# Order of the score products inside one attention item of a decoder-layer kernel

## The chip, the cores and the metric

One core of a Trainium2 chip runs the whole kernel. The time is in device microseconds (us) of one execution; the kernel before was run three times for its median, and one further execution was taken by the hardware profiler. All rows below come from that profiled execution.

## What is computed

One decoder layer for a prompt of 2048 tokens (width 1024) and a small sample group. The part that matters here is the dilated attention of the prompt: 8 heads of 64 dimensions, three patterns `p` (dilation 1, 4 and 16). In each pattern a block of 128 queries sees its own block of 128 keys and, where there is one, the block before:

```python
scores = jnp.einsum('bnqchd,bnkchd->bnchqk', qb, kb).astype(jnp.float32) * (HEAD_DIM ** -0.5)
scores = jnp.where(valid[None, :, None, None], scores + bias[None, None, None], NEG)
m = jnp.max(scores, axis=-1, keepdims=True)
p = jnp.exp(scores - m)
l = jnp.sum(p, axis=-1, keepdims=True)
out = jnp.einsum('bnchqk,bnkchd->bnqchd', (p / l).astype(v.dtype), vb)
```

Before it come the input projection, norms and the pooling mixer; after it the merge of the patterns, the output projection and a convolutional feed-forward network (up-projection, convolution, down-projection).

## The kernel before, in words

The kernel runs in stages: projection, then attention, then output projection, then the feed-forward network. Attention is cut into 192 **items**, 24 for each head (eight for each pattern). An item `(h, p, pr)` is two query blocks, `s = 0` and `s = 1`. Both write into one PSUM tile `Sp` of 128 x 2 x 256 fp32 values, one half for each `s`. A half is 256 wide where the block has an earlier block of keys and 128 wide where it has none; these are called wide and narrow here. The queries of patterns 1 and 2 are copied beforehand into `qs` by GpSimd (L241).

Three functions issue the work of an item, and `advance(i)` (the body of the loop over items) calls them for three different items: `scores` of item i, `turn` of item i - 2, `values` of item i - 3. So a result of `scores` is first needed by TensorE two items later.

- `scores` (L275 to L296): for each half two products into `Sp`, with the high (L289) and the low part (L290) of the keys; then one VectorE instruction (L292) that adds the bias table, writes `T` and takes the row minimum into `st` (with a short second instruction that reads the accumulator); then the exponential on ScalarE (L294) into `Pt`.
- `turn` (L298 to L309): a transpose on TensorE (L302) for each 128 x 128 block of `Pt`, two to four in an item, into a PSUM tile `tp`, then one copy to SBUF, `PTs`: on VectorE (L305) three times of four, on ScalarE (L307) the fourth.
- `values` (L311 to L333): for each block a product of `PTs` with the values (L324, two instructions in the trace for each one in the code); after every second item a ScalarE copy of the result (L328), and a store of `O` to DRAM after each group of four (L227 to L233).

The first eight items are issued while the stage before ends, and the scheduler of the framework may reorder them. All others stand in a loop under `tc.manual_schedule()`, which keeps the order of the program on every engine. The framework adds the semaphores by itself and follows the use of tiles. `Sp` has four buffers, `T` three, `Pt` three, `tp` and `Op` share four, `PTs` has four.

In the same loop the SyncE queue (SP) issues loads: keys and queries of the next head (L161 to L166), values (L185, L193), and late in the stage eight pieces of the output weights, `rawo` (L737), each of which is split by ScalarE (L112) and VectorE (L113) right where it stands in the program order; the first stands at item 150, the sixth of head 6.

Of the kernel before, what the change touches and what calls it, by code (L numbers as in the profile page):

```python
# [47 lines left out]
def kernel(ctx, tc, ins, cst, outs):  # L48
# [212 lines left out]
    def views(h, p, idx):  # L261
        r = DILS[p]
        blk, c = divmod(idx, r)
        lo = blk - 1 if blk else 0

        def keys(x):
            if p == 0:
                return x[:, lo * P:(blk + 1) * P]
            return x.rearrange("p (m c i) -> p m c i", c=r, i=RUN)[:, lo * P // RUN:(blk + 1) * P // RUN, c, :]

        return queries(h, p, idx), keys(heads[h][1]), keys(heads[h][2]), ([idx - r] if blk else []) + [idx]
# [3 lines left out]
    def scores(it):  # L275
        h, p, pr = it
        tab = heads[h][3]
        if pr % 4 == 0:
            state["st", p] = pq.tile([P, 8], F32, tag="st", name="st", bufs=8)
        st = state["st", p]  # L280
        Sp = psum.tile([P, 2, 2 * P], F32, tag="mm", name="Sp", bufs=4)
        Pt = pq.tile([P, 2, 2 * P], F32, tag="P", name="Pt", bufs=3)
        blocks = []
        for s in range(2):
            idx = 2 * pr + s
            i8 = idx % 8
            q, kh, kl, kb = views(h, p, idx)
            w = P * len(kb)
            nc.tensor.matmul(Sp[:, s, :w], q, kh, start=True, stop=False)  # L289
            nc.tensor.matmul(Sp[:, s, :w], q, kl, start=False, stop=True)  # L290
            T = pq.tile([P, 2 * P], F32, tag="T", name="T", bufs=3)
            nc.vector.tensor_tensor_reduce(out=T[:, :w], in0=Sp[:, s, :w], in1=tab[:, p, 2 * P - w:], op0=ALU.add,  # L292
                                           op1=ALU.min, scale=1.0, scalar=3e38, accum_out=st[:, i8:i8 + 1])
            nc.scalar.activation(Pt[:, s, :w], T[:, :w], AF.Exp, bias=st[:, i8:i8 + 1], scale=-1.0)  # L294
            blocks += [(s, idx % 4, n, b, len(kb)) for n, b in enumerate(kb)]
        return st, Pt, blocks  # L296

    def turn(it, res):  # L298
# [57 lines left out]
    def advance(i):  # L356
        if i >= AHEAD:
            spread_next(i + SPREAD)
        if i < len(items):
            attn[i] = scores(items[i])  # L360
        if 0 <= i - 2 < len(items):
            PTs[i - 2] = turn(items[i - 2], attn[i - 2])
        if 0 <= i - 3 < len(items):
            values(items[i - 3], attn.pop(i - 3), PTs.pop(i - 3))
# [380 lines left out]
    with tc.tile_pool(name="p4", bufs=1, reuse_waits="tile") as p4:  # L745
# [102 lines left out]
        for gi, grp in enumerate(groups):  # L848
# [22 lines left out]
            for i, t in enumerate(grp):  # L871
# [4 lines left out]
                if i >= late and nxt:  # L876
                    n = nxt[i - late]
# [243 lines left out]
        for c in range(NCHUNK):  # L1121
            last = c == NCHUNK - 1
            T = TM if last else CH
            spans = [(0, T // 2), (T // 2, T // 2)] if last else [(0, CH)]
            nt = 5 if last else 4

            def spread(pss, prompt, sample):

                if not last:
                    return [(prompt, pss[0])]  # L1130
                h = T // 2
                return [(prompt[:, 0:h], pss[0][:, :h]), (prompt[:, h:CH], pss[1][:, :CH - h]),
# [52 lines left out]
            def up_pair(i, slot, act):  # L1185
                gt = conv_tile(i)
                vt = conv_tile(NF + i)
                sg = p4.tile([P, TM], F32, tag="cv", name="sg", bufs=4)
                nc.scalar.activation(sg[:, :T], gt[:, :T], AF.Silu)
                nc.vector.tensor_tensor(out=vt[:, :T], in0=vt[:, :T], in1=sg[:, :T], op=ALU.mult)  # L1190
# [102 lines left out]
```

## Time and profile before

| what | value |
|---|---|
| median of 3 runs | 2927.72 us (2925.48 to 2929.7) |
| profiled execution, its own time | 2930.08 us |
| its span, first to last instruction | 2928.3 us |
| mean granted TensorE clock over the span | 0.874 of full speed |
| busy: TensorE, VectorE, ScalarE, GpSimd | 2762.1, 1750.5, 1108.0, 184.3 us |
| attention loop, from the trace | about 466 to 1176 us of the span |

A busy time is the union of an engine's instructions. The ends of matmuls are modelled and overlap the next one's start, so the distance between the starts of two matmuls is the better measure of what one costs. [...] PE is TensorE, PEld its weight loads, DVE VectorE, ACT ScalarE, POOL GpSimd.

### The profile page before, as it was taken

The page shows a single profiled execution, that of the slowest core. Times are in us where ns is not written, and L with a number is a line of the kernel's source. Part 1 is how long each engine was busy: PE and PEld are TensorE (multiplying, and loading weights), DVE is VectorE, ACT ScalarE, POOL GpSimd, SP SyncE. Part 2 cuts the span into 40 slices and gives each one's busy share as a digit, 9 for nine tenths or more (in the row PEclk, how much of TensorE's full clock was granted, in tenths as well). Part 3 has the DMA queues.
Part 4 walks back from the last instruction along what each step waited for, and adds up shares of the span by engine and source line. Part 5 has one row for each costly group of instructions (what it writes and reads, how often), then busy time and mean ns, then how long its engine had stood idle before and what let it go on. Part 6 is the DMA issues. An engine that isn't in the chain of part 4 may idle for free.

```text
span 2928.3 us, 36228 instructions
## 1 busy us (share of the span) xinstructions
PE 2762.1 (94%) x13310; PEld 2355.7 (80%) x13310; DVE 1750.5 (60%) x3819; ACT 1108.0 (38%) x2021; POOL 184.3 (6%) x246
## 2 busy tenths in 40 slices
PE   7999997888888687999999999999999999999999
PEld 5888887777777676787788888888888888999998
DVE  6444453333333233676889887888888766666665
ACT  5333333333333233222533434544444444444442
POOL 1111121111011110100000000000000000000000
PEclk9999996555555555999999999999999999999999
DMA  6333335332223411797855565344564344522221
GB/s 201 112 125 112 105 109 146 87 90 45 78 56 81 105 40 37 260 315 251 246 186 176 168 206 183 109 134 144 184 193 129 117 128 140 179 82 87 88 84 58
DMA packets 412877, 393.60 MB, mean 134 GB/s; under 512 B 16347, under 2 KB 319543, under 8 KB 410012
## 3 DMA queue, kind: packets, MB, share of 16 engines
q1 hardware_dynamic: 412476, 390.48, 43.6%
q8 instruction: 105, 1.72, 0.2%
q0 software_dynamic: 224, 0.80, 0.1%
q14 instruction: 72, 0.59, 0.1%
HBM read 305.70 MB, written 85.52 MB: 134 GB/s over the span
## 4 chain that ended last, share of the span: by engine, by line
PE 88%; DVE 4%; issue 3%; DMA 3%; POOL 1%; SPq 0%; ACT 0%; DVEq 0%; POOLq 0%; ACTq 0%
PE pu L1037 34%; PE pd L1213 17%; PE ps L470 11%; PE Op L324 7%; PE po L816 5%; PE Sp L289 5%; PE tp L302 4%; PE Sp L290 3%; DVE T L292 2%; PE tp L122 1%; PE tp L479 1%; PE pd L1207 1%; DMA rawo<-in_w_out_dram 1%; DMA QK<-kT_lo 1%; PE pp L551 0%
## 5 line engine op out<-in xcount | busy, mean ns | idle before, releaser
L1037 PE MATMUL pu<-h,w 128*128 128x512 f32 (+1 forms) x5232 | 990.6, 350 | 2.1 <-ACT w L112 1.6
L1037 PEld LDWEIGHTS pu<-h,w 128*128 128x128 f32 x5232 | 851.0, 188 | 133.4 <-ACT w L112 2.0
L1213 PE MATMUL pd<-w,act 128*128 128x512 f32 x2112 | 490.2, 392 | 0.0
L1213 PEld LDWEIGHTS pd<-w,act 128*128 128x128 f32 x2112 | 396.6, 188 | 88.1
L112 ACT CAST w<-raw 128x1024 fp32r<-128x1024 f32 (+1 forms) x282 | 287.0, 1026 | 292.2 <-PE pd L1213 186.2
L292 DVE CUSTOM_DVE_ANT_0 T<-Sp,tab 128x256 f32<-128x256 f32 (+1 forms) x384 | 140.1, 366 | 421.6 <-PE Sp L290 414.2
L113 DVE TENSOR_TENSOR w<-raw,w 128x1024 fp32r<-128x1024 f32 (+1 forms) x278 | 328.9, 1186 | 24.9 <-ACT w L112 24.8
L470 PE MATMUL ps<-W_hi,xh 128*128 128x512 f32 x1024 | 333.0, 398 | 1.0 <-ACT xh L112 1.0
L294 ACT ACTIVATE Pt<-T,st 128x256 f32<-128x256 f32 (+1 forms) x384 | 176.6, 462 | 411.4 <-DVE st L292 411.4
L1181 DVE SCALAR_TENSOR_TENSOR cv<-ex,cw,cv 128x512 f32<-128x512 f32 x352 | 262.3, 745 | 28.9 <-ACT cv L1173 26.3
L324 PEld LDWEIGHTS Op<-V,PTs 128*128 128x128 f32 x1200 | 273.0, 326 | 0.1
L324 PE MATMUL Op<-V,PTs 128*128 128x65 f32 x1200 | 269.2, 394 | 0.0
L1171 ACT COPY ex<-pu 128x512 f32<-128x512 f32 (+1 forms) x220 | 110.1, 500 | 345.4 <-PE pu L1037 345.2
L470 PEld LDWEIGHTS ps<-W_hi,xh 128*128 128x128 f32 x1024 | 192.7, 189 | 43.2 <-ACT xh L112 1.5
L470 PE MATMUL ps<-W_lo,xh 128*128 128x512 f32 x512 | 202.7, 396 | 0.0
L289 PE MATMUL Sp<-QK,qs 128*128 128x128 f32 (+1 forms) x256 | 128.9, 504 | 74.4 <-DVE st L292 74.4
L1215 DVE TENSOR_TENSOR ya<-ya,pd 128x512 f32<-128x512 f32 x192 | 131.0, 684 | 103.3 <-PE pd L1213 102.6
L95 POOL TENSOR_TENSOR rs<-ms,mhalf 128x8 f32<-128x8 f32 (+3 forms) x68 | 76.4, 1124 | 1588.9 <-DVE stT L1174 1048.8
L302 PE MATMUL tp<-ident,Pt 128*128 128x128 f32 x600 | 166.0, 415 | 0.0
L1173 ACT ACTIVATE cv<-pu,cw 128x512 f32<-128x512 f32 (+3 forms) x264 | 166.0, 649 | 0.0
L289 PEld LDWEIGHTS Sp<-QK,qs 128*128 128x128 f32 x256 | 78.7, 308 | 104.1 <-DVE st L292 103.7
L289 PE MATMUL Sp<-QK 128*128 128x256 f32 (+1 forms) x128 | 69.6, 550 | 61.3 <-DVE st L292 56.7
(225 smaller groups left out, 2905.9 us busy)
## 6 DMA issues: line engine op xcount, KB each, us to landing
raw<-in_w_up_dram SPq DMA_DIRECT2D x176, 512.0 KB
raw<-in_w_down_dram SPq DMA_DIRECT2D x80, 512.0 KB
hn_s<-w SPq DMA_DIRECT2D x16, 1024.0 KB
h<-hn_s SPq DMA_DIRECT2D x32, 512.0 KB
far<-in_cache_k_dram SPq DMA_DIRECT2D x64, 256.0 KB
far<-in_cache_v_dram SPq DMA_DIRECT2D x64, 256.0 KB
om<-o_s SPq DMA_DIRECT2D x16, 792.0 KB
raw<-in_w_in_dram SPq DMA_DIRECT2D x16, 512.0 KB
```

What stands on the lines that cost most here:

```text
L112: nc.scalar.copy(hi, src)
L113: (eng or nc.vector).tensor_tensor(out=lo, in0=src, in1=f32(hi), op=ALU.subtract)
L289: nc.tensor.matmul(Sp[:, s, :w], q, kh, start=True, stop=False)
L292: nc.vector.tensor_tensor_reduce(out=T[:, :w], in0=Sp[:, s, :w], in1=tab[:, p, 2 * P - w:], op0=ALU.add, op1=ALU.min, scale=1.0, scalar=3e ...
L294: nc.scalar.activation(Pt[:, s, :w], T[:, :w], AF.Exp, bias=st[:, i8:i8 + 1], scale=-1.0)
L302: nc.tensor.transpose(tp[:, j, :], Pt[:, s, n * P:(n + 1) * P], ident)
L324: nc.tensor.matmul(Op[:, i4, :], PT[:, j, :], pair_v[hp, p, b][:, v0:v0 + DH + 1], start=n == 0, stop=n == m - 1)
L470: nc.tensor.matmul(ps, xh[:, a, k, :], (W_hi, W_lo)[b][j, k // 2][:, k % 2, :], start=n == 0, stop=n == 3 * KT - 1)
L1037: nc.tensor.matmul(ps[:, :n], w[:, a, k, :], hs[k][:, b, c0:c0 + n], start=i == 0, stop=i == 3 * KT - 1)
L1173: nc.scalar.activation(d, s, AF.Identity, bias=cw[:, 3, ct:ct + 1], scale=cw[:, 2, ct:ct + 1])
L1181: nc.vector.scalar_tensor_tensor(out=d, in0=e[j], scalar=cw[:, j, ct:ct + 1], in1=d, op0=ALU.mult, op1=ALU.add)
L1213: nc.tensor.matmul(ps, act[0][:, a, k, tau * P:(tau + 1) * P], wd[k][:, b, :], start=k == 0 and j == 0, stop=k == n - 1 and j == 2)
```

## The change

In `scores`, the loop over the two halves is split in two. The first loop issues the four score products of the item, the second the two bias instructions and the two exponentials. Nothing else differs: the same instructions with the same operands, the same tiles and buffers.

```diff
-        blocks = []
+        blocks, parts = [], []
         for s in range(2):
             idx = 2 * pr + s
-            i8 = idx % 8
             q, kh, kl, kb = views(h, p, idx)
             w = P * len(kb)
             nc.tensor.matmul(Sp[:, s, :w], q, kh, start=True, stop=False)
             nc.tensor.matmul(Sp[:, s, :w], q, kl, start=False, stop=True)
+            parts.append((s, idx % 8, w))
+            blocks += [(s, idx % 4, n, b, len(kb)) for n, b in enumerate(kb)]
+        for s, i8, w in parts:
             T = pq.tile([P, 2 * P], F32, tag="T", name="T", bufs=3)
             nc.vector.tensor_tensor_reduce(out=T[:, :w], in0=Sp[:, s, :w], in1=tab[:, p, 2 * P - w:], op0=ALU.add,
                                            op1=ALU.min, scale=1.0, scalar=3e38, accum_out=st[:, i8:i8 + 1])
             nc.scalar.activation(Pt[:, s, :w], T[:, :w], AF.Exp, bias=st[:, i8:i8 + 1], scale=-1.0)
-            blocks += [(s, idx % 4, n, b, len(kb)) for n, b in enumerate(kb)]
         return st, Pt, blocks
```

## Rows read from the trace of the kernel before

**Rows 1.** The page: busy time of TensorE; its granted clock in 40 slices.

```profile
PE 2762.1 (94%) x13310; PEld 2355.7 (80%) x13310; DVE 1750.5 (60%) x3819; ACT 1108.0 (38%) x2021; POOL 184.3 (6%) x246
...
PEclk9999996555555555999999999999999999999999
```

**Rows 2.** Windows: stretch and length, busy us (instructions) by engine, PEclk, DMA.

```profile
452.00:455.80 3.80, 3.80 (x18) 3.41 (x18) 1.85 (x9) 2.19 (x5) 0.00 (x0) 0.50 0.50 158
456.00:459.00 3.00, 3.00 (x29) 2.97 (x27) 2.65 (x10) 1.98 (x5) 0.48 (x9) 1.00 0.67 193
466.10:1176.00 709.90, 580.32 (x2479) 532.97 (x2480) 222.62 (x898) 224.25 (x515) 85.94 (x148) 0.50 0.28 70
684.00:688.00 4.00, 3.48 (x16) 3.48 (x16) 1.56 (x5) 1.02 (x2) 0.20 (x1) 0.50 0.00 0
1176.10:1180.00 3.90, 3.90 (x37) 3.85 (x35) 1.95 (x5) 1.36 (x3) 0.20 (x1) 1.00 0.24 69
```

**Rows 3.** Waits of TensorE, 466.1 to 1176 us: total us, times, longest.

```profile
PE Sp L289 <- DVE st L292: 130.4, 184, 15.1
```

**Rows 4.** Timeline, a wide item at 707 us: start, duration, instruction, [idle before].

```profile
707.26 0.41 PE L290 MATMUL Sp<-QK 128*128 128x256 f32 x1
...
708.31 0.58 PE L289 MATMUL Sp<-QK 128*128 128x256 f32 x1 [0.64 <-DVE st L292]
...
708.69 0.42 PE L290 MATMUL Sp<-QK 128*128 128x256 f32 x1
...
709.26 0.42 DVE L292 CUSTOM_DVE_ANT_0 T<-Sp,tab 128x256 f32<-128x256 f32 x1 [1.00 <-PE Sp L290]
...
709.61 0.08 DVE L292 DVE_READ_ACCUMULATOR2_ANT st<- 128x1 f32 x1
709.73 0.51 ACT L294 ACTIVATE Pt<-T,st 128x256 f32<-128x256 f32 x1 [0.93 <-DVE st L292]
```

**Rows 5.** Timeline of TensorE, a narrow item at 542 us.

```profile
541.54 0.41 PE L290 MATMUL Sp<-QK,qs 128*128 128x128 f32 x1
542.46 0.47 PE L289 MATMUL Sp<-QK,qs 128*128 128x128 f32 x1 [0.50 <-DVE st L292]
```

**Rows 6.** Timeline of TensorE among the first eight items, score products back to back.

```profile
450.71 0.41 PE L290 MATMUL Sp<-QK 128*128 128x256 f32 x1
450.92 0.41 PE L289 MATMUL Sp<-QK 128*128 128x256 f32 x1
451.14 0.41 PE L290 MATMUL Sp<-QK 128*128 128x256 f32 x1
```

**Rows 7.** Groups by line and shape, 466.1 to 1176 us: count, busy us, mean ns.

```profile
L324 PE MATMUL Op<-V,PTs 128*128 128x65 f32 x1130 | 259.7, 401 | 0.0
L302 PE MATMUL tp<-ident,Pt 128*128 128x128 f32 x565 | 159.1, 422 | 0.0
...
L292 DVE CUSTOM_DVE_ANT_0 T<-Sp,tab 128x256 f32<-128x256 f32 x202 | 85.8, 425 | 235.9 <-PE Sp L290 231.1 <-POOL qs L241 3.9 <-issue 0.9
...
L305 DVE COPY PTs<-tp 128x512 f32<-128x512 f32 x82 | 56.7, 692 | 32.2 <-PE tp L302 32.2
...
L292 DVE CUSTOM_DVE_ANT_0 T<-Sp,tab 128x128 f32<-128x128 f32 x167 | 48.7, 291 | 172.8 <-PE Sp L290 170.2 <-ACT O L328 2.6
```

**Rows 8.** Timeline of TensorE at the end of the stage, at the high clock.

```profile
1176.45 0.28 PE L290 MATMUL Sp<-QK 128*128 128x256 f32 x1
1176.57 0.60 PE L302 MATMUL tp<-ident,Pt 128*128 128x128 f32 x4
1177.01 1.00 PE L324 MATMUL Op<-V,PTs 128*128 128x65 f32 x8
1177.85 0.39 PE L302 MATMUL tp<-ident,Pt 128*128 128x128 f32 x2
```

**Rows 9.** Timeline of SP and ACT around the first load of output weights.

```profile
985.89 4.76 SPq L231 DMA_DIRECT2D o_s<-O  x2
...
1014.47 0.62 ACT L112 CAST h<-rawo 128x512 fp32r<-128x512 f32 x1 [14.21 <-DMA rawo<-in_w_out_dram]
```

## The prediction

> **What bounds the kernel now.** I read the page first. TensorE is busy for 94% of the span, and its clock is granted in full except in ten slices from the seventh on, where it falls to about half [rows 1]. Those slices are the attention stage, so that is where to look. [...] Only TensorE is near its limit, and it has two kinds of loss: it idles, and it runs at the lower of its two levels. The waits name the idle part: 130.4 us in 184 waits of the first product of a half (L289) for the `st` of a bias (L292) [rows 3]. There are 369 biases, so 184.5 items [rows 7]: this wait comes once in each item. The timeline shows which it is. The second half's product starts at 708.31, right after the first half's bias, though it writes other columns; it waits because both halves are one tile [rows 4]. 709.9 us over 184.5 items is 3.85 us an item.
>
> **The change part by part.** *Removed: the wait inside an item.* In a wide item the second half's first product starts 1.05 us after the product before it (707.26 to 708.31), and its own successor 0.38 us later [rows 4]. Back to back, a product follows the one before by 0.21 us [rows 6]. So a wide item saves 0.84 + 0.17 = 1.0 us. In a narrow one the first distance is 0.92 us [rows 5] and becomes 0.21: 0.71 us. With 202 / 2 = 101 wide and 167 / 2 = 83.5 narrow items [rows 7] this is 101 + 59 = 160 us, if the clock stays as it is. (The 130.4 us of the waits hold the idle alone, one of 15.1 us among them that a DMA causes and that stays; the rest of the 160 is what modelled ends and exposed weight loads hide.)
>
> *Added: the first bias starts after the fourth product and not after the second,* two products or 0.42 us later at the low level. Behind it on VectorE stand the second bias and the copy of an older transpose (L305); ScalarE's exponentials follow. I cost this at nothing, because TensorE needs `Pt` only two items later. From the start of the last product it takes 0.57 us to the bias, 0.35 to the next instruction, 0.12 to the exponential, 0.51 for it [rows 4]; with a second bias of 0.35 in between that is 1.9 us, against 2 x 2.9 us of TensorE's work. The cover is thinner at the high level; see below. The order on VectorE and ScalarE does not change, no DMA is moved, and SP and POOL issue what they did, only as fast as buffers come free. The first eight items may be ordered anew, at no cost: their products stand together already [rows 6].
>
> *Moved: the clock.* This term decides, and the trace holds no stretch of steady items without the wait, so I bound it. One end is no change of the level: 160 us. The other is the high level for all of it. The nearest rows are the first items, which ran without program order. From 452.0 to 455.8 TensorE ran wide score products, transposes and value products without a gap, 3.80 us of 3.80, at 0.50; from 456 on the clock was 1.00 [rows 2]. No other kind of work had come between. Against it: from 684 to 688 it was busy for 3.48 us of 4.00, and the clock stayed at 0.50 [rows 2]. There it ran one wait, then eight value products in a row with few score products. The changed order lacks the wait, and puts four score products together, so in items that follow short transposes it resembles the first stretch. That row is the nearer, and I take the high level.
>
> At that level the end of the stage shows the prices: 0.12 us for a score product, 0.44 for four transposes, 0.84 for eight value instructions [rows 8]. Four score products I put at 0.56 us (4 x 0.12, and 0.08 for the first one's exposed weight load, half of the 0.17 above). The sum, with the counts of [rows 7]:
>
> - scores 184.5 x 0.56 = 103 us; transposes 565 x 0.11 = 62; values 1130 x 0.105 = 119; together 284 us or 1.54 us an item.
> - New waits at this pace, 37 us (0.2 an item, between 0 and 0.4). In a full wide item the copy that the value products need is done about 0.57 + 2 x 0.35 + 0.08 + 0.69 = 2.04 us after the last score product starts [rows 4, 7], and TensorE comes to them after 0.12 + 0.44 + 0.84 + 0.56 + 0.44 = 2.40. That holds, but with 0.36 to spare, and less where a narrow item with half the transposes and values stands between.
> - The first load of output weights, 24 us. From the last store of the head before (985.89), through other loads in the same queue, to the split on ScalarE (1014.47) it takes 28.6 us [rows 9]. That is DMA time and does not shrink, while the items that cover it do: three of them by then, 3 x 1.54 us. It stalls TensorE for 15.1 us now [rows 3] and for 24 then.
> - Stretches at the low level at the start and after that stall, 15 us (5 to 25; an estimate from the gap-free stretch before the rise in [rows 2], which ran low for several us).
>
> Together 284 + 37 + 24 + 15 = 360 us in place of 709.9: 350 us less. The profiled execution took 2930.08 us (span 2928.3), so 2580; the median of the runs is 2.4 us below it, which gives **2578 us**.
>
> [...]
>
> **The rivals.**
> 1. *The clock stays at 0.50.* For it: 684 to 688 [rows 2], and 710 us of this work without a rise. Against it: the rise at 456. Only the wait is saved: 2930.1 - 160 - 2.4 = 2768 us. Chance 0.07.
> 2. *The clock changes to and fro,* high for about half of the stage, because stalls and runs of narrow items send it down. Midway: about 2670 us. For it: the 15.1 us wait [rows 3] and the queue of [rows 9] repeat at head boundaries. Against it: at 1176 to 1180 the same work holds 1.00 [rows 2]. Chance 0.10.
> 3. *Slower: a wait at the transposes takes the place of the one removed.* The first bias now waits for all four products, so `Pt` comes later; if the chain from the last product to the second exponential took longer than two items of TensorE's work, every L302 would wait for the rest. The point from which that costs more than it saves is a chain of over 2 x 3.85 = 7.7 us, four times the 1.9 us worked out above. At 0.1 us more than now for each of 184.5 items it would be 2928 + 18 = 2946 us. Against it: [rows 4], where such a chain is short. Chance 0.03.
> 4. *Nothing happens,* because the second half's product waits for something else that ends at the same time. Then 2928 us. Against it: in [rows 6] four such products stand 0.21 us apart with no bias between. Chance 0.02.
>
> **How the numbers follow.** The forecast has a chance of 0.78. Its own range is 2530 (no new waits, 5 us at the low level: 37 + 10 less) to 2630 (0.4 us an item, 25 us). The unknown price is the clock's, with both ends in the chances, so the range reaches from there to the first rival: 2530 to 2770. A measurement of this kernel tells about 0.2% from no change. Faster by more: 0.78 + 0.10 + 0.07 = 0.95; within it 0.02; slower 0.03.
>
> **What the profile after would show.** Right: the waits of L289 for L292 gone but for those that a DMA causes; four score products of an item 0.1 to 0.2 us apart; the first bias after the fourth; PEclk at 1.00 from early in the stage; items of about 1.7 to 1.8 us; a wait of over 20 us for `rawo`; a stage of some 360 us and a DMA share near 0.55. The later stages should keep their lengths. Wrong in size: PEclk at 0.50 with TensorE gap-free (first rival), or PEclk mixed. Wrong in kind: TensorE waiting at L302 for L294, or at L324 for L305, in every item and by more than a few tenths of a us; or a wait for `QK` or `V` loads at each head, which would say that the DMA queue now sets the pace.

## The result, and the profile after

The changed kernel takes 2559.27 us (median of four runs, 2556.24 to 2564.7) against 2926.66 for the kernel before (median of four): a ratio of 0.8745, with a 95% interval from 0.8729 to 0.8762. The forecast was 2578 us and the range 2530 to 2770.

The page of the changed kernel answers to [rows 1]. (The functions behind `scores` moved down by one line; in `scores` the products are now L288 and L289, the bias L294, the exponential L296.)

```profile
PE 2486.2 (97%) x13310; PEld 2119.1 (83%) x13310; DVE 1725.1 (67%) x3819; ACT 1079.1 (42%) x2021; POOL 186.6 (7%) x246
...
PEclk9999999899978999999999999999999999999999
```

The ten slices at half clock are gone. TensorE's busy time fell by 276 us with the same 13310 instructions, as the slices in which it fell to half clock now show the full one. The windows answer to [rows 2]; the last row is the kernel after attention.

```profile
462.70:480.80 18.10, 18.09 (x87) 17.80 (x87) 7.10 (x39) 8.04 (x23) 3.47 (x5) 0.50 0.62 154
490.00:690.00 200.00, 196.12 (x1696) 189.57 (x1696) 130.50 (x603) 128.17 (x340) 60.90 (x108) 1.00 0.69 163
702.70:736.80 34.10, 12.74 (x60) 12.75 (x61) 7.30 (x30) 7.44 (x19) 1.75 (x5) 0.50 0.54 122
811.00:2557.00 1746.00, 1733.12 (x8648) 1457.57 (x8647) 1303.69 (x2402) 710.18 (x1177) 21.34 (x22) 1.00 0.51 161
```

The stage starts at the low level, with TensorE busy in all of 18.1 us, goes to 1.00 at about 481 us and stays there until a stall at 700. The same stretch of 1746 us at the end took as long before the change (TensorE busy for 1731.7 us of it, at 1.00): the whole gain lies in the attention stage. Its last score product starts at 806.7 us; before, at 1176.5.

The next rows show two wide items in the timeline of TensorE: the four score products of one at the low level (from 477.94 us), and a longer part of one at the high level:

```profile
477.94 0.56 PE L288 MATMUL Sp<-QK,qs 128*128 128x256 f32 x1
478.30 0.41 PE L289 MATMUL Sp<-QK,qs 128*128 128x256 f32 x1
478.51 0.41 PE L288 MATMUL Sp<-QK,qs 128*128 128x256 f32 x1
478.73 0.41 PE L289 MATMUL Sp<-QK,qs 128*128 128x256 f32 x1
...
561.58 0.36 PE L288 MATMUL Sp<-QK 128*128 128x256 f32 x1
561.78 0.28 PE L289 MATMUL Sp<-QK 128*128 128x256 f32 x1
561.90 0.28 PE L288 MATMUL Sp<-QK 128*128 128x256 f32 x1
562.02 0.28 PE L289 MATMUL Sp<-QK 128*128 128x256 f32 x1
562.13 0.60 PE L303 MATMUL tp<-ident,Pt 128*128 128x128 f32 x4
562.98 0.77 PE L325 MATMUL Op<-V,PTs 128*128 128x65 f32 x5 [0.24 <-ACT PTs L308]
```

At the low level the second half's first product follows after 0.21 us, where it followed after 1.05 [rows 4], and its successor after 0.22, where it was 0.38: the 1.0 us of the prediction. At the high level the three distances are 0.20, 0.12 and 0.12 us. The last row shows a new, small wait: that of the value products for a transposed tile that ScalarE copies. In all, from 462 to 812 us, TensorE's waits were these two, with count and longest:

```profile
PE Op L325 <- ACT PTs L308: 28.5, 14, 24.1
PE Op L325 <- DVE PTs L306: 8.1, 4, 5.6
```

Nothing is left of the 130.4 us of [rows 3]. The longest wait, 24.1 us, is the first load of output weights. The timeline of SP, ACT and TensorE there answers to [rows 9]:

```profile
695.50 1.24 SPq L231 DMA_DIRECT2D o_s<-O  x2
...
707.04 15.78 SPq L738 DMA_DIRECT2D rawo<-in_w_out_dram  x3
...
721.12 0.62 ACT L112 CAST h<-rawo 128x512 fp32r<-128x512 f32 x1 [22.55 <-DMA rawo<-in_w_out_dram]
...
724.05 0.69 PE L325 MATMUL Op<-V,PTs 128*128 128x65 f32 x2 [24.14 <-ACT PTs L308]
```

From the last store of the head before to the split it took 25.6 us (28.6 before): DMA time, which the faster items no longer cover.

### The profile page after: what moved, and what is told of

Same layout as the page of the kernel before. It is cut to its first block, busy times and chain, and to the rows that moved or that the text cites. A ratio compares the mean times of both kernels' runs of the same rounds, so it can differ in the third digit from the quotient of the medians.

```text
span 2557.5 us, 36059 instructions
## 1 busy us (share of the span) xinstructions
PE 2486.2 (97%) x13310; PEld 2119.1 (83%) x13310; DVE 1725.1 (67%) x3819; ACT 1079.1 (42%) x2021; POOL 186.6 (7%) x246
## 4 chain that ended last, share of the span: by engine, by line
PE 66%; DMA 1%; DVE 1%; issue 0%; ACT 0%; SPq 0%; POOL 0%; DVEq 0%; POOLq 0%; ACTq 0%
PE pu L1038 38%; PE pd L1214 19%; PE po L817 5%; PE pd L1208 1%; PE tp L122 0%; DMA raw<-in_w_out_dram 0%; PE Op L325 0%; DMA raw<-in_w_up_dram 0%; PE sacc L990 0%; PE sacc L989 0%; PE po L1071 0%; DVE at L796 0%; PE tpa L802 0%; DMA h_s<-ya 0%; PE tpf L1106 0%
## 5 line engine op out<-in xcount | busy, mean ns | idle before, releaser
L296 ACT ACTIVATE Pt<-T,st 128x256 f32<-128x256 f32 (+1 forms) x384 | 157.0, 456 | 130.0 <-DVE st L294 128.0
L325 PE MATMUL Op<-V,PTs 128*128 128x65 f32 x1200 | 168.7, 281 | 37.0 <-ACT PTs L308 28.5
L294 DVE CUSTOM_DVE_ANT_0 T<-Sp,tab 128x256 f32<-128x256 f32 (+1 forms) x384 | 125.0, 364 | 118.0 <-PE Sp L289 78.7
L325 PEld LDWEIGHTS Op<-V,PTs 128*128 128x128 f32 x1200 | 159.7, 203 | 44.8 <-ACT PTs L308 35.3
L112 ACT CAST act<-cv 128x512 fp32r<-128x512 f32 x88 | 54.6, 620 | 162.5 <-DVE cv L1191 156.3
L471 PEld LDWEIGHTS ps<-W_lo,xh 128*128 128x128 f32 x512 | 96.8, 189 | 19.8
L1175 DVE COPY stT<-ex 128x2 f32<-128x2 f32 x176 | 28.8, 163 | 117.0 <-ACT ex L1172 117.0
L303 PE MATMUL tp<-ident,Pt 128*128 128x128 f32 x600 | 103.8, 286 | 0.0
```

The source lines that it names most:

```text
L112: nc.scalar.copy(hi, src)
L325: nc.tensor.matmul(Op[:, i4, :], PT[:, j, :], pair_v[hp, p, b][:, v0:v0 + DH + 1], start=n == 0, stop=n == m - 1)
L471: nc.tensor.matmul(ps, xh[:, a, k, :], (W_hi, W_lo)[b][j, k // 2][:, k % 2, :], start=n == 0, stop=n == 3 * KT - 1)
```

## The experiments

My theory: the wait inside an item cost twice, as idle time and because TensorE, with a gap in each item, stayed at a granted clock of 0.50. It is the missing wait that counts, not the order of the products as such. Rivals: the clock rises because four products stand together; or the waits alone make the gain and the clock has no part in it.

**The wait removed without the order.** Each half gets a score tile of its own; the order in the program is that of the kernel before.

```diff
-        Sp = psum.tile([P, 2, 2 * P], F32, tag="mm", name="Sp", bufs=4)
+        Sp = [psum.tile([P, 2 * P], F32, tag="mm", name="Sp", bufs=4) for _ in range(2)]
...
-            nc.tensor.matmul(Sp[:, s, :w], q, kh, start=True, stop=False)
-            nc.tensor.matmul(Sp[:, s, :w], q, kl, start=False, stop=True)
+            nc.tensor.matmul(Sp[s][:, :w], q, kh, start=True, stop=False)
+            nc.tensor.matmul(Sp[s][:, :w], q, kl, start=False, stop=True)
...
-            nc.vector.tensor_tensor_reduce(out=T[:, :w], in0=Sp[:, s, :w], in1=tab[:, p, 2 * P - w:], op0=ALU.add,
+            nc.vector.tensor_tensor_reduce(out=T[:, :w], in0=Sp[s][:, :w], in1=tab[:, p, 2 * P - w:], op0=ALU.add,
```

> [...] If the wait between the halves is what the change removes, and it came from the shared tile: waits of the score products for the bias nearly gone, the clock at 1.00 for most of the stage, and 2560 us, give or take 25 (the first bias even starts two products earlier, but there are buffers for two items ahead only, in place of four). If it is the burst of four products that raises the clock, and not the missing wait: the wait gone, the clock at 0.50, about 2768 us.

Measured: 2552.91 us, ratio 0.8725 (0.871 to 0.8739). The clock on its page:

```profile
PEclk9999999899978999999999999999999999999999
```

Three of TensorE's waits from 440 to 810 us:

```profile
PE Op L324 <- ACT PTs L307: 25.6, 6, 24.4
PE Op L324 <- DVE PTs L305: 8.2, 4, 5.5
...
PE Sp L289 <- DVE st L292: 0.3, 1, 0.3
```

The wait is gone with the old order, and the time is that of the changed kernel or a little below. So the wait came from the shared tile: 115.3 us of it with one tile (130.4 less the 15.1 that a DMA causes [rows 3]), 0.3 with two. About the burst of four products this run decides nothing, though the expectation takes it so. By the code, neither the change nor this edit moves an instruction within the order of its own engine; they alter what waits for what. Without the wait the four products stand together in this run too:

```profile
560.33 0.31 PE L289 MATMUL Sp<-QK,qs 128*128 128x128 f32 x1
560.48 0.28 PE L290 MATMUL Sp<-QK,qs 128*128 128x128 f32 x1
560.59 0.28 PE L289 MATMUL Sp<-QK,qs 128*128 128x128 f32 x1
560.70 0.28 PE L290 MATMUL Sp<-QK,qs 128*128 128x128 f32 x1
```

The next two experiments separate the burst from the wait.

**The wait kept, but filled.** Order and waits of the kernel before; two spare products stand in the gap.

```diff
+            if s == 0 and state["i"] >= AHEAD:
+                state["tp"] = psum.tile([P, 4, P], F32, tag="tp", name="tp2", bufs=4)
+                for _ in range(2):
+                    nc.tensor.matmul(state["tp"].rearrange("p a b -> p (a b)"), q, heads[h][1][:, 0:CH], start=True, stop=True)
             T = pq.tile([P, 2 * P], F32, tag="T", name="T", bufs=3)
...
```

(The lines left out set `state["i"]` to the number of the item and let `turn` write its transposes into this same tile afterwards.)

> The order and the wait of the kernel before, with two spare products of 512 columns put into the wait of each item (work added, written to a transpose tile that is overwritten later). At the low level they take about as long as the wait. If the clock follows whether TensorE runs without gaps: it rises, the wait then shows again behind the shorter spare products, an item takes about 1.54 + 0.8 = 2.3 us, the stage some 470 us, the kernel about 2690 us. If the gain of the change came from the waits alone, or the clock needs the four products together: 2930 us, the clock at 0.50.

Measured: 2684.17 us in a single run (before: 2928.33, median of seven runs from 2923.45 to 2930.22). The next two experiments, and those with wide or narrow items alone, are single runs too. A window of the stage, and TensorE in one wide item there:

```profile
480.00:790.00 310.00, 296.98 (x2056) 238.87 (x2054) 153.91 (x640) 153.37 (x362) 65.35 (x117) 1.00 0.48 115
```

```profile
561.31 0.28 PE L290 MATMUL Sp<-QK 128*128 128x256 f32 x1
561.42 0.63 PE L294 MATMUL tp<-QK 128*128 128x512 f32 x2
562.22 0.39 PE L289 MATMUL Sp<-QK 128*128 128x256 f32 x1 [0.17 <-DVE st L296]
```

Work was added, every wait for a bias is still in the program (0.91 us from product to product), and the kernel is 244 us faster. The clock stands at 1.00 for 310 us, with two spare products between the score products of the two halves: it rises without the burst of four. The 244 us are what the high level gives with the waits left in the program. The other 125 us, from 2684 to 2559, are what the wait, with the spare products in it, costs at the high level.

**The wait moved to another place.** The changed order, and then one spare transpose that needs this item's first bias.

```diff
             nc.scalar.activation(Pt[:, s, :w], T[:, :w], AF.Exp, bias=st[:, i8:i8 + 1], scale=-1.0)
+            if s == 0:
+                state["T"] = T
...
         tp = psum.tile([P, 4, P], F32, tag="tp", name="tp2", bufs=4)
+        if "T" in state:
+            nc.tensor.transpose(tp[:, 0, :], state.pop("T")[:, 0:P], ident)
```

> The changed order, with a wait put back in another place: before the transposes of the older item TensorE does one spare transpose of the sum that this item's first bias has just written (work added, overwritten by the real transpose). If TensorE's wait in each item is what matters, wherever it stands: the clock stays at 0.50, an item takes about 4.0 us, the kernel about 2950 us. If the order of the products matters by itself: the clock rises, an item takes about 2.4 us, the kernel about 2710 us.

Measured: 2935.65 us. Two windows, TensorE's one kind of wait from 496 to 1185 us, and its timeline in one narrow item:

```profile
520.00:1000.00 480.00, 407.69 (x1792) 375.75 (x1792) 137.38 (x594) 136.07 (x334) 60.77 (x112) 0.50 0.27 68
466.00:490.00 24.00, 17.99 (x146) 16.22 (x144) 10.94 (x53) 10.41 (x29) 5.83 (x8) 1.00 0.77 178
```

```profile
PE tp L305 <- DVE st L294: 122.3, 170, 14.2
```

```profile
703.24 0.45 PE L288 MATMUL Sp<-QK,qs 128*128 128x128 f32 x1
703.49 0.41 PE L289 MATMUL Sp<-QK,qs 128*128 128x128 f32 x1
703.71 0.41 PE L288 MATMUL Sp<-QK,qs 128*128 128x128 f32 x1
703.92 0.41 PE L289 MATMUL Sp<-QK,qs 128*128 128x128 f32 x1
704.93 0.45 PE L305 MATMUL tp<-ident,T 128*128 128x128 f32 x1 [0.59 <-DVE st L294]
```

The four products stand together here as in the changed kernel, and nothing is gained: with the burst in place the clock stood at 0.50. The stage even began at 1.00; TensorE was busy for 18 us of 24 there, with 11 waits for the bias, then the clock fell (at about 496 us) and did not come back for 690 us. This is rival 3 of the prediction made on purpose: a wait at the transposes takes the whole gain back.

**The new order in every second item.**

```diff
+        new = pr % 2 == 1
...
+            if new:
+                parts.append((s, idx % 8, w))
+            else:
+                bias(s, idx % 8, w)
+        for part in parts:
+            bias(*part)
```

(`bias` is a function made of the three lines with `T`, the bias and the exponential. The next two experiments have the same edit with another condition for `new`.)

> The changed order in every second item, the order before in the others. If the clock stays at 0.50 with half of the waits: half of 160 us is saved, about 2850 us. If it rises: items of 1.54 and 2.3 us in turn, the stage some 400 us, about 2620 us. If the clock had no part in the gain: half of the whole gain, 2743 us, at a clock like that of the kernel before.

Measured: 2691.9 us. The clock went to and fro, as these windows show:

```profile
466.00:535.00 69.00, 62.89 (x286) 60.40 (x286) 23.06 (x105) 24.40 (x62) 13.57 (x16) 0.50 0.50 111
540.00:670.00 130.00, 109.56 (x894) 102.32 (x894) 71.75 (x316) 72.79 (x178) 30.01 (x59) 1.00 0.55 137
680.00:740.00 60.00, 54.36 (x247) 51.83 (x246) 20.66 (x87) 20.44 (x49) 9.27 (x13) 0.50 0.28 60
```

None of the three expected times came. The busy share of a stretch does not tell its level in these runs: 0.84 at 1.00 here from 540 to 670, and 0.85 at 0.50 in the run with the moved wait.

**The new order in wide items alone** (`new = 2 * pr >= DILS[p]`) **and in narrow items alone** (`new = 2 * pr < DILS[p]`).

> The changed order in the wide items alone; the narrow ones keep their wait. If the clock stays at 0.50: 101 of the 160 us are saved, 2828 us. If gap-free wide items raise it and it then holds through the narrow ones: 83.5 waits of about 0.64 us at the high level, 2613 us. A time between says that it changes to and fro, as in the run with every second item.

> The changed order in the narrow items alone; the wide ones keep their wait. If the clock stays at 0.50, as it did in the changed kernel while TensorE ran narrow items without a gap from 466 to 478 us: 59 of the 160 us are saved, 2870 us. If any work without gaps raises it: 101 waits of about 0.78 us at the high level, 2640 us.

Measured: 2663.61 and 2845.45 us. Their clocks:

```profile
PEclk9999999797876799999999999999999999999999
```

```profile
PEclk9999997555555557999999999999999999999999
```

With the new order in the wide items the clock rises, but with the waits of the narrow ones in place it falls again and again (1.00 from 690.4 to 744.9 us, 0.50 from 772.4 to 809.7). With the new order in the narrow ones it hardly rises: 470 to 840 us stood at 0.50. The time is 25 us below what I expected for a low clock. Two stretches of 10 us each at 1.00 (844.7 to 855 and 861.7 to 872 us) can have saved at most as much time again, 20 us, and the wait for the first weights was 17.6 us, longer than before (15.1); so some of the 25 us stays unexplained.

**The weights later.** The eight pieces of output weights move from items 150 to 185 to items 166 to 187, in the changed kernel, in the kernel before, and in the kernel with two tiles. The changed kernel ran beside them once more.

```diff
-                    if i >= 150 and i % 5 == 0 and i < 190:
-                        k = ((i - 150) // 5 + 4) % KT
+                    if i >= 166 and i % 3 == 1 and i < 188:
+                        k = ((i - 166) // 3 + 4) % KT
```

> The changed kernel as it is, once more, to stand beside the next three on the same chip: 2559 us, give or take 6.

> The changed kernel, with the eight loads and splits of output weights moved from items 150 to 185 (every fifth) to items 166 to 187 (every third). If the 24 us of waiting in the middle of the stage is the DMA time of the loads ahead of the first piece, which the faster items no longer cover: sixteen items of 1.6 us cover it, the wait goes, and with it about half of the 14 us of work at the lower clock behind it, 2528 us. If that wait only moves to the later pieces, which now stand closer together: 2559 us.

> The same move of the output weights in the kernel before the change. There the wait is 15.1 us and the clock is low before and after it, so only the wait goes: 2912 us. If the move is worth as much here as in the changed kernel, the price of the load does not depend on the pace of the items: about 2898 us.

> The old order with a score tile for each half, and the output weights moved to items 166 to 187. If the two edits act on different things: 2553 - 31 = 2522 us. If the faster stage is held by the DMA queue by now: no better than the changed kernel with the late weights alone.

Measured: the changed kernel 2561.49 us (ratio 0.875, 0.8737 to 0.8763); with late weights 2541.27 (0.8684, 0.8671 to 0.8697); the kernel before with late weights 2917.1 (0.997, 0.9958 to 0.9983); two tiles and late weights 2537.53 (0.8675, 0.8658 to 0.8693). TensorE's waits in the changed kernel with late weights, 455 to 810 us:

```profile
PE Op L325 <- ACT PTs L308: 9.7, 16, 4.3
PE Op L325 <- DVE PTs L306: 7.9, 4, 4.6
PE Sp L288 <- DMA QK<-kT_hi: 6.5, 2, 3.6
```

The wait of 24.1 us is gone. The gain is 20 us and not 31: two waits of over 4 us at the later pieces remain, and after them the clock fell for short stretches (754 to 771, 785 to 792 us; two others were shorter). The same move is worth 9.5 us in the kernel before, where the wait was 15.1 us and one of 5.7 us remains. So the price of that load did rise with the pace, as the prediction had it. The best of these versions, two tiles with late weights, stands at 2537.5 us, not at the 2522 of two gains added; its interval overlaps that of the changed kernel with late weights, so the two tiles add nothing there that these runs can tell.

## Why the prediction was right, and what it missed

- **What bounds the kernel**: right. Removing TensorE's wait or filling it moved the time by hundreds of us, with VectorE and ScalarE busy for 0.69 of a stretch at most (137.2 and 133.3 us of 200 with two tiles, 130.5 and 128.2 in the changed kernel). Before, TensorE was busy for 0.82 of the stage's 709.9 us, VectorE and ScalarE for 0.31 and 0.32 [rows 2].
- **The wait, 160 us at a fixed clock**: the distances came out as worked out, at the low level in the changed kernel itself (0.21 us and 0.22).
- **The clock**: right in what decided. Most of a stage that had stood at 0.50 ran at 1.00, and with the waits filled but kept that is worth 244 us. The row I took as the nearer one, 452 to 456 us, was the nearer. Nearly a fourth of the instructions were transposes (384 of 1696 from 490 to 690 us), and the clock stood at 1.00 for these 200 us. What the level goes by is not settled, and the gap in each item is not the whole of it. Here TensorE worked without a gap from 462.7 to 480.8 us at 0.50, on narrow items first, and the rise came in the second of the wide items that follow. In the run with the moved wait it waited in each of 11 items from 466 to 490 us (6.0 us in all) and stayed at 1.00. Shown is less: over hundreds of us of steady items the level was low where each item had its gap (the kernel before, the moved wait) and high where the gap was gone or filled.
- **The later first bias, costed at nothing**: right to under 10 us. With two tiles the first bias starts earlier (in a narrow item 0.57 us after the item's first product, 560.33 to 560.90 us; in the changed kernel 0.82, 566.11 to 566.93), and the kernel is 6 to 9 us faster, at the edge of the intervals; the waits for a transposed tile without the two that a DMA causes are 3.9 us there (25.6 + 8.2 - 24.4 - 5.5) and 6.9 here (28.5 + 8.1 - 24.1 - 5.6).
- **New waits at the higher pace, 37 us**: the term that was mis-sized. It measured 6.9 us, 0.04 an item. Only 2.5 us of it, in three waits, are behind copies on VectorE, the path for which the margin of 0.36 us was worked out. The other 4.4 us, in thirteen waits, are behind copies on ScalarE, a path that the working left out.
- **The first load of weights, 24 us**: 24.1, in part by luck. From the store to the split it took 25.6 us, 3.0 less than in the row of before; from the split to TensorE's next product it took another 2.9 us (721.12 to 724.05), which the sum had left out. The two cancel. A second wait of 5.6 us, at a later piece, was not in the sum.
- **Stretches at the low level, 15 us**: about 22. TensorE worked for 18.1 + 12.7 us at 0.50 at the start and after the stall, and for 13.5 us more in two short stretches near the end of the stage (771.0 to 777.8 us, and 791.4 to 801.7 with a part of the 5.6 us wait in it). At the high level it would have needed about half of these 44 us, an estimate from the same work at both levels: eight value instructions took 1.56 us at 464.01 and 0.82 at 803.68.
- **An item without waits, 1.54 us**: about 1.58. From 490 to 690 us there are 248 biases, so 124 items, at 1.61 us each, of which 0.03 are waits; 0.04 over 184.5 items is 8 us more.
- **Balance**: new waits 30 us less; low stretches 7, the second wait 6 and the items themselves 8 more. That leaves 9 us below the forecast, where the run was 19 below; 5.5 us of the rest are an earlier start, which the sum did not have (the last score product of the loop's first item starts at 462.67 us, before at 468.22); the other 3 to 4 I cannot place. That the sum came so near is in part luck, since 30 us too much and 21 too little nearly cancel. Terms of a few us also differ from run to run: in the second profile of the changed kernel (2557.55 us, against 2559.28) that product starts at 465.48 us, and TensorE worked at 0.50 for 35 us from 440 to 810 us, against 49.

The rivals: none of them happened in the changed kernel, but the second is what half a change gives (every second item, wide items alone), and the third what a wait at the transposes gives. The row held against the second rival, 1176 to 1180 us, is not the same work: its last score product starts at 1176.45 [rows 8], and only transposes and value products follow.

## What to carry to other kernels

When a stage runs at half of TensorE's clock, price a wait of TensorE twice: the idle time at the present level, and the whole stage at the other level; here the second was the larger (244 us, against 125 for the wait at the high level). Look at what the wait is for before reordering: here a shared tile made two independent halves wait, and a tile for each did the same as the new order (2553 us, against 2559). Once a stage is twice as fast, find the transfers that its length used to cover: here the wait for the first weights went from 15.1 to 24.1 us.

## What the runs showed that I had not expected

Useless work made the kernel faster: two spare products in each item, 244 us less, with the clock at 1.00 in place of 0.50. And half of a change may be worth more or less than half of its gain: the new order in every second item brought 236 of 367 us, in wide items 264, in narrow items 82, and the last two together less than the whole (346), as in each of these runs the clock stood at 1.00 for a part of the stage only.
